# Output projection by one level of Strassen's product, in a gated parallel hybrid encoder layer

## The chip, the cores and the metric

The kernel runs on one core of one Trainium2 chip. The metric is the device time of one execution in microseconds; of several runs the median is given. The profile is that of one execution, and its span reaches from the first to the last instruction.

## The reference, cut to what matters

The layer works on x of 1024 tokens by 1024 channels in float32. One combined projection of the normed x feeds five branches (neighbourhood attention, differential attention, pooling, spatial gating, memory attention) and five gates per channel. The gated branches are summed and pass one output projection:

```python
h = rmsnorm(x, norm_g)
proj = h @ w_in
...
merged = jnp.zeros_like(x)
for i, y in enumerate((y_a, y_b, y_c, y_d, y_m)):
    g_logit = proj[..., SLAB_COLS + i * D_MODEL: SLAB_COLS + (i + 1) * D_MODEL] + b_gate[i]
    merged = merged + jax.nn.sigmoid(g_logit.astype(jnp.float32)).astype(x.dtype) * (y @ w_branch[i])
return x + merged @ w_out
```

So merged and w_out are both 1024 by 1024, and the last product is one of three of that kind of size (the input projection is nine times as wide).

## The kernel before

Every matrix product is made of three: each operand is cut into a coarse part (a cast to fp32r on ScalarE) and a fine part (the difference, on VectorE), and coarse x coarse, coarse x fine and fine x coarse are added in PSUM. `split` does this for activations, `split_w` for weights, in pieces of 128x512.

The normed x is kept transposed in SBUF, in the tiles hh and hl (coarse and fine). `norm_T` makes it by token tiles of 128: load, sum of squares on ScalarE, a reciprocal root by Newton steps on VectorE (`rsqrt_col`), scaling, eight transposes on TensorE, cuts. The weights of w_in come in blocks of 256 columns. Two blocks are held at a time in the slots of wh and wl; `load_w` fills a slot in four pieces as soon as the block before it in this slot has been used. The first two blocks are loaded whole.

The order of the work is the list ORDER of named units, written by hand. A unit emits its instructions; a dash after its name emits the next stage of the same unit. For each engine a scheduler then fixes one fixed queue: it takes the units' position as a priority and goes by its own estimate of when inputs are ready. All loads and stores go from SP's queue, in order, apart from four setup loads on GpSimd's. Units named here: `ld` and `wk` load and norm a token tile, `gn` spreads the norm's gain, `su` is the setup of constants, `bqk`, `bv` are projections of the differential attention, `s` are gate units whose result goes to DRAM early (fillers for TensorE), `mq`, `ma` belong to the memory attention, `g` are the last gate units, which sum a branch into acc.

After the fifth branch of a pair of channel tiles, `merge` cuts acc into mh and ml. Then `out_proj` makes 16 tiles of 128 tokens by 512 columns, each of 8 channel tiles x 3 = 24 matmuls of 128x512, adds x and writes the tile. The left half of w_out is loaded into the two slots (blocks WO0 and WO1), the right half by `load_wo` into the tiles hh0 and hl0, which are free by then; its pieces are cut by ScalarE and VectorE as the first tiles are computed.

## Time and profile before

| | |
|---|---|
| runs, us | 1226.64, 1229.48, 1233.31 |
| median, us | 1229.48 |
| profiled execution, us | 1229.92 |
| its span, us | 1228.1 |
| TensorE, VectorE, ScalarE, GpSimd busy | 98%, 59%, 42%, 12% of the span |
| mean granted clock of TensorE | 0.999 |
| HBM read and written | 103.56 MB and 47.19 MB |

PE is TensorE, PEld its weight loads, DVE VectorE, ACT ScalarE, POOL GpSimd, SP the queue that issues most DMAs. Matmuls overlap, so the busy time of one is longer than the distance from one to the next. Idle time of an engine that is not the bottleneck costs nothing by itself.

### The profile page before, as it was taken

What the parts mean: (1) busy time and instruction counts of PE and PEld (TensorE: products, weight loads), DVE (VectorE), ACT (ScalarE), POOL (GpSimd) and SP (SyncE); (2) the same over time, 40 slices, a digit from 0 to 9 for tenths busy, and PEclk for the clock granted to TensorE, in tenths of its full rate; (3) what the DMA queues carried; (4) which work ended last, traced back from release to release, by engine and by line L of the source; (5) the groups of instructions that cost most, each with busy time, mean ns of one, the idle gap of its engine ahead of it and who ended that gap; (6) DMA issues with size and microseconds to landing.
All of it is one profiled execution on the core that took longest, in us unless ns stands there. A gap on an engine that the chain in (4) does not pass through costs nothing.

```text
span 1228.1 us, 17866 instructions
## 1 busy us (share of the span) xinstructions
PE 1201.9 (98%) x6680; PEld 1031.9 (84%) x6680; DVE 721.5 (59%) x1557; ACT 511.3 (42%) x1033; POOL 144.9 (12%) x150
## 2 busy tenths in 40 slices
PE   7999999999999999999999999999999999999998
PEld 5988888898888898987888898788987777888787
DVE  6865766654476668746655566546555537457411
ACT  5545555434365554334436545535354421113200
POOL 1001111100011111104000001301000004323000
PEclk9999999999999999999999999999999999999999
DMA  6022222113222222333222315835565679562321
GB/s 238 1 87 69 71 74 73 41 48 100 69 80 65 83 86 80 102 107 105 79 86 74 108 44 188 270 129 193 158 218 172 209 267 371 209 232 73 124 97 69
DMA packets 71162, 151.91 MB, mean 124 GB/s; under 512 B 8226, under 2 KB 9794, under 8 KB 71076
## 3 DMA queue, kind: packets, MB, share of 16 engines
q1 hardware_dynamic: 70884, 150.31, 36.4%
q8 instruction: 52, 0.85, 0.3%
q0 software_dynamic: 192, 0.47, 0.1%
q14 instruction: 34, 0.28, 0.1%
HBM read 103.56 MB, written 47.19 MB: 123 GB/s over the span
## 4 chain that ended last, share of the span: by engine, by line
PE 86%; DMA 5%; DVE 4%; ACT 3%; issue 1%; SPq 0%; POOL 0%; DVEq 0%; ACTq 0%; POOLq 0%
PE g L363 15%; PE g L364 15%; PE g L365 15%; PE gz L1000 6%; PE g L349 5%; PE g L351 5%; PE g L350 5%; DMA wr<-in_w_in_dram 3%; PE s L471 3%; PE po L508 2%; PE aT L497 2%; PE g L1090 2%; PE g L1091 2%; PE g L1089 2%; PE ao L906 1%
## 5 line engine op out<-in xcount | busy, mean ns | idle before, releaser
L363 PE MATMUL g<-hh,wh 128*128 128x512 f32 x864 | 342.4, 397 | 3.5 <-ACT gth L984 1.2
L364 PE MATMUL g<-hh,wl 128*128 128x512 f32 x864 | 340.9, 395 | 0.2 <-DVE wl L337 0.2
L365 PE MATMUL g<-hl,wh 128*128 128x512 f32 x864 | 340.8, 394 | 0.0
L363 PEld LDWEIGHTS g<-hh,wh 128*128 128x128 f32 x864 | 162.6, 188 | 35.4 <-ACT gth L984 1.4
L365 PEld LDWEIGHTS g<-hl,wh 128*128 128x128 f32 x864 | 162.6, 188 | 31.8
L364 PEld LDWEIGHTS g<-hh,wl 128*128 128x128 f32 x864 | 162.7, 188 | 31.2 <-DVE wl L337 0.5
L337 DVE TENSOR_TENSOR wl<-wr,wh 128x512 fp32r<-128x512 f32 x148 | 110.9, 753 | 84.8 <-ACT wh L336 84.4
L336 ACT CAST wh<-wr 128x512 fp32r<-128x512 f32 x148 | 91.6, 620 | 156.5 <-DMA wr<-in_w_in_dram 114.9
L349 PE MATMUL g<-wh,hh 128*128 128x256 f32 x512 | 146.9, 288 | 2.6 <-ACT hh L199 1.6
L351 PE MATMUL g<-wh,hl 128*128 128x256 f32 x512 | 146.7, 288 | 0.1
L350 PE MATMUL g<-wl,hh 128*128 128x256 f32 x512 | 146.0, 287 | 0.0
L349 PEld LDWEIGHTS g<-wh,hh 128*128 128x128 f32 x512 | 98.7, 193 | 4.3 <-ACT hh L199 2.7
L1000 PE MATMUL gz<-yh,wb 128*128 128x512 f32 x320 | 100.1, 393 | 2.2 <-DVE gtl L1052 1.9
L351 PEld LDWEIGHTS g<-wh,hl 128*128 128x128 f32 x512 | 98.5, 193 | 1.2 <-issue 0.8
L350 PEld LDWEIGHTS g<-wl,hh 128*128 128x128 f32 x512 | 98.6, 193 | 0.5
L984 ACT ACTIVATE gth<-g,pc 128x512 f32<-128x512 f32 x80 | 55.0, 688 | 99.5 <-PE g L365 76.5
L479 ACT ACTIVATE pB<-s,bmx 128x1024 f32<-128x1024 f32 x64 | 71.6, 1119 | 40.1 <-DVE bmx L477 35.5
L477 DVE TENSOR_REDUCE bmx<-s 128x1 f32<-128x1024 f32 x64 | 77.4, 1217 | 15.2 <-PE s L471 13.0
L485 POOL TENSOR_SCALAR pB<-pB,brc 128x1024 f32<-128x1024 f32 x32 | 38.0, 1189 | 303.6 <-DVE brc L484 196.2
L1000 PEld LDWEIGHTS gz<-yh,wb 128*128 128x128 f32 x320 | 59.3, 188 | 16.0 <-DVE gtl L1052 2.7
L928 POOL TENSOR_TENSOR yy<-yy,yz 128x512 f32<-128x512 f32 x20 | 26.7, 1336 | 332.3 <-DMA yz<-sz 89.1
L1000 PE MATMUL gz<-yl,wb 128*128 128x512 f32 x160 | 62.4, 390 | 0.0
(240 smaller groups left out, 1797.6 us busy)
## 6 DMA issues: line engine op xcount, KB each, us to landing
wr<-in_w_in_dram SPq DMA_DIRECT2D x132, 256.0 KB, 3.4
gs<-gth SPq DMA_DIRECT2D x52, 256.0 KB, 2.0
gtl<-gs SPq DMA_DIRECT2D x26, 512.0 KB, 4.5
wx<-we SPq DMA_DIRECT2D x14, 512.0 KB, 4.0
wb<-wx SPq DMA_DIRECT2D x14, 512.0 KB, 5.7
yx<-ye SPq DMA_DIRECT2D x12, 512.0 KB, 4.3
sz<-zt SPq DMA_DIRECT2D x20, 256.0 KB, 2.0
yz<-sz SPq DMA_DIRECT2D x20, 256.0 KB, 4.1
```

The source lines that it names most:

```text
L336: nc.scalar.copy(out=hi.bitcast(F32R), in_=src)
L337: nc.vector.tensor_tensor(out=lo.bitcast(F32R), in0=src, in1=hi, op=ALU.subtract)
L349: nc.tensor.matmul(out=ps[:, t, :], lhsT=hh[:, ts], rhs=a, start=(i == 0), stop=False)
L350: nc.tensor.matmul(out=ps[:, t, :], lhsT=hh[:, ts], rhs=b, start=False, stop=False)
L351: nc.tensor.matmul(out=ps[:, t, :], lhsT=hl[:, ts], rhs=a, start=False, stop=(i == KT - 1))
L363: nc.tensor.matmul(out=ps, lhsT=a, rhs=hh[:, ts], start=(k == 0), stop=False)
L364: nc.tensor.matmul(out=ps, lhsT=b, rhs=hh[:, ts], start=False, stop=False)
L365: nc.tensor.matmul(out=ps, lhsT=a, rhs=hl[:, ts], start=False, stop=(k == KT - 1))
L477: nc.vector.tensor_reduce(out=nmx[:, m:m + 1], in_=ps, axis=AX.X, op=ALU.max, negate=True)
L479: nc.scalar.activation(out=pe, in_=ps, func=AF.Exp, bias=nmx[:, m:m + 1], accum_out=sums[:, m:m + 1])
L984: nc.scalar.activation(out=tn, in_=ps, func=AF.Tanh, bias=self.bg[:, br, j:j + 1], scale=0.5)
L1000: self.nc.tensor.matmul(out=pz[:, ts], lhsT=wb[:, a, k, cs].bitcast(F32R), rhs=y[b][k][:, ts].bitcast(F32R), start=(i == 0), stop=(i == 5))
```

## The change

The output projection is computed as seven products of half size (Winograd's form of one level of Strassen's scheme), for tokens and output columns in halves, with the channels in halves too. The left operands of four products are sums of quarters of merged, made on VectorE (`s_sums`, and cuts in `sb`, `sd`, `se`) after the last gate unit, in the tiles that h has left. The right operands of four products are sums of quarters of w_out; `t_early` (units wt0 to wt3) makes and cuts them during the memory attention and stores them in DRAM, and `load_o` reads them back. Each product has four tiles of 128x512 with 4 x 3 = 12 matmuls. The units q1, q2, q6, q7, q5, q4, q3 run in this order; P2, P4 and P3 are accumulated in PSUM on top of P1, P7 and P5, and the sums of products are made by VectorE and GpSimd. The stores of the output are issued by ScalarE.

At the start, the fine parts of the first two weight blocks are made by GpSimd (`cut`, units c0 to c7), the setup loads (`sud`) are a unit of their own ahead of the setup's arithmetic, the gain's load goes from ScalarE's queue, and `wk`, `bqk0` and `bv` are divided into more stages. The rest of ORDER is rearranged; `v0.1` is gone, so that these weights are cut when they are used, and `v1.3` is new. The units first, warm0 to warm2 and wp0 to wp7 are defined but do not stand in ORDER. m_norm works its two tiles as one.

```diff
-h ld0 gn ld1 ld2 wk0 id wk0' wk1 L wk1' su ld3 wk3 bst0 ld4 wk2 bvt L wk2' ld5 bqk0.0 wk3' ld6 wk5 wk4 bqk0.0' bv.0
...
-g0.3.1 wo op0.0 op1.0 op0.1 op0.2 op0.4 op1.5 op0.7 op0.6 op1.3 op1.2 op0.5 op0.3 op1.4 op1.6 op1.7 op1.1
+h gn ld0 ld1 wk0 L ld2 wk0' id wk1 wk0'' wk0''' wk1' wk2 c0 c1 c2 c3 sud ld3 wk3 wk1'' ld5 wk1''' bqk0.0 wk3' wk2' su
+bqk0.0' L c4 c5 c6 bvt wk3'' c7 bst0 ld4 wk2'' wk5 ld6 wk2''' wk3''' wk4 bqk0.0'' wk4' wk5' bv.0 bv.0' wk4'' wk4'''
+wk5'' ld7 bqk0.1 wk6 bqk0.1' wk5''' wk6' wk6'' wk6''' wk7 bv.1 wk7' bv.2 bv.1' wk7'' wk7''' bqk0.2 bqk0.2' bv.2'
+bqk0.2'' bqk0.3 bqk0.3' bv.3 bqk0.3'' bv.3' bqk0.1'' s4.2.1.1 ba0.0 ba0.0' ba0.1 ba0.0'' s2.1.0.1 s4.2.0.1 ba0.0'''
...
+du.1 bs0.1' du.3 s4.1.1.0 bs1.1 cl0 bs1.1' dm mn' cl1 ch0 co0 mk co0' ch1 mk' mv co1 mq.0 s0.0.0.1 wt0 mq.1 co1'
+s0.0.1.0 mq.0' avt mq.1' mq.2 mq.2' s0.0.0.0 wt1 mq.3 mq.3' s0.0.1.1 wt2 ma0.0 ma0.1 ma0.0' ma0.0'' av.0.0 ma0.1'
+s0.1.0.0 wt3 av.0.1 ma1.0 s0.1.0.1 ma1.0' ma1.0'' ma2.0 u3.1.0 ma1.1 ma1.1' s0.1.1.0 avx0 ma1.1'' ma0.1'' ma2.0' ma2.1
...
+g2.0.1 w2.2 w2.3 g2.0.0 y4 g2.1.1 g2.2.0 g2.2.1 g2.3.0 w0.2 w4.0 g2.1.0 w4.1 w0.3 g4.0.1 g4.0.0 w4.2 g2.3.1 g4.1.0
+g4.2.0 w4.3 g4.1.1 g4.3.0 w0.0 y0 g4.3.1 w0.1 g0.0.1 g0.1.0 g4.2.1 g0.0.0 g0.1.1 g0.2.0 g0.3.0 g0.2.1 g0.3.1 q1.0 q1.1
+q1.2 q1.3 o6 sa q2.0 q2.1 q2.2 q2.3 sb q6.0 q6.1 q6.2 q6.3 o4 q7.0 q7.1 q7.2 q7.3 sd q5.0 q5.1 q5.2 q5.3 se q4.0 q4.1
+q4.2 q4.3 q3.0 q3.1 q3.2 q3.3
...
+    def setup_loads(self):
+        nc, io, c = self.nc, self.io, self.const
         bc = self.btile("bc")
         cc = self.page("cc")
         nc.gpsimd.dma_start(out=cc[:, 0:384], in_=io["c_mix"])
...
         self.ce = c([P, 32], F32, "ce")
         nc.gpsimd.dma_start(out=self.ce, in_=io["c_edge"])
+        self.early = bc, pv, cc
+
+    def setup(self):
...
-            nc.sync.dma_start(out=row[0:1, :], in_=g.rearrange("(o d) -> o d", o=1))
+            (nc.scalar if early else nc.sync).dma_start(out=row[0:1, :], in_=g.rearrange("(o d) -> o d", o=1))
...
+        def work(i, n=1):
+
+            ss = self.small(n, f"xss{n}")
+            xs, xns = [st.pop(i + j) for j in range(n)], [self.page("xn") for _ in range(n)]
+            for j in range(n):
+                nc.scalar.activation(out=xns[j], in_=xs[j], func=AF.Square, accum_out=ss[:, j:j + 1])
             yield
...
+            r = self.rsqrt_col(ss, n, 1.0 / D, EPS)
+            for j in range(n):
+                nc.vector.scalar_tensor_tensor(out=xns[j], in0=xs[j], scalar=r[:, j:j + 1], in1=st["g"], op0=ALU.mult,
+                                               op1=ALU.mult)
+                yield
+            for j, xn in enumerate(xns):
+                cs = slice((i + j) * P, (i + j + 1) * P)
+                for q in range(2):
+                    ps = self.tbank("xT")
+                    for c in range(4):
+                        k = q * 4 + c
+                        nc.tensor.transpose(out=ps[:, c * P:(c + 1) * P], in_=xn[:, k * P:(k + 1) * P],
+                                            identity=self.ident)
+                    self.split(hi[q][:, :, cs], lo[q][:, :, cs], ps.rearrange("p (a b) -> p a b", a=4))
+                    yield
...
-            v = self.vbig("wv").rearrange("p (k c) -> p k c", k=KT)
+            v = self.big("wv").rearrange("p (k c) -> p k c", k=KT)
         for q in range(4):
             ks = slice(q * 2, q * 2 + 2)
             r = v[:, ks] if whole else self.raw("wr").rearrange("p (k c) -> p k c", k=2)
             nc.sync.dma_start(out=r, in_=src[:, ks])
-            self.split_w(wh[:, ks, :], wl[:, ks, :], r)
+            if whole:
+                self.cuts.append((wh[:, ks, :], wl[:, ks, :], r))
+            else:
+                self.split_w(wh[:, ks, :], wl[:, ks, :], r)
...
+    def cut(self, i):
+        hi, lo, src = self.cuts[i]
+        self.nc.scalar.copy(out=hi.bitcast(F32R), in_=src)
+        self.nc.gpsimd.tensor_tensor(out=lo.bitcast(F32R), in0=src, in1=hi, op=ALU.subtract)
...
         ps = self.gemm_tok(w, tp)
+        if hp == 0:
+            yield
...
+    def b_v(self, w, tp):
+        ps = self.gemm_tok(w, tp)
+        yield
+        for pr in range(2):
+            self.v_split(self.bvt[pr][:, tp * 2:tp * 2 + 2], ps[:, :, pr * P:(pr + 1) * P])
...
+        self.mrg += [(2 * jp + jj, self.acc[jp][:, jj]) for jj in range(2)]
+        for _, a in self.mrg[-2:]:
+            u = self.unit("m1").rearrange("p (x t) -> p x t", x=2)
+            self.s_cut(u, a[:, 0:512])
+            self.m1.append((u[:, 0], u[:, 1]))
+
+    def s_sums(self):
+
+        nc = self.nc
+        self.S = [self.hp.tile([P, 2, 4, 512], F32, name=f"S{i}", tag=t) for i, t in
+                  enumerate(("hh0", "hl0", "hh1", "hl1"))]
+        for k in range(4):
+            a, b = self.mrg[k][1], self.mrg[4 + k][1]
+            a0, a1, b0, b1 = a[:, 0:512], a[:, 512:T], b[:, 0:512], b[:, 512:T]
+            tt = lambda o, x, y, op: nc.vector.tensor_tensor(out=o, in0=x, in1=y, op=op)
+            s1, s2 = self.tmp("s1"), self.ftmp("s2")
+            tt(s1, a1, b1, ALU.add)
+            tt(s2, s1, a0, ALU.subtract)
+            tt(a1, a0, a1, ALU.subtract)
+            tt(a0, b0, s2, ALU.subtract)
+            self.s_cut(self.S[1][:, :, k], s2)
+            self.s_cut(self.S[0][:, :, k], s1)
+
+    def s_cut(self, out, src):
+
+        nc = self.nc
+        nc.scalar.activation(out=out[:, 0].bitcast(F32R), in_=src, func=AF.Copy, scale=0.25)
+        nc.vector.scalar_tensor_tensor(out=out[:, 1].bitcast(F32R), in0=src, scalar=0.25, in1=out[:, 0], op0=ALU.mult,
+                                       op1=ALU.subtract)
+
+    def a22(self, k):
+        u = self.unit("m2").rearrange("p (x t) -> p x t", x=2)
+        self.s_cut(u, self.mrg[4 + k][1][:, 512:T])
+        self.m2.append((u[:, 0], u[:, 1]))
+
+    def t_early(self, k):
+
+        nc = self.nc
+        r = [self.unit("tr").rearrange("p (c n) -> p c n", c=2) for _ in range(2)]
+        for row in range(2):
+            for col in range(2):
+                nc.sync.dma_start(out=r[row][:, col], in_=self.io["w_out"][col][:, self.rows_of[row * 4 + k]])
+        (b11, b12), (b21, b22) = [[x[:, c] for c in range(2)] for x in r]
+        sub = lambda o, x, y: nc.vector.tensor_tensor(out=o, in0=x, in1=y, op=ALU.subtract)
+
+        def out(i, x):
+            u = self.unit("to").rearrange("p (x n) -> p x n", x=2)
+            self.split_w(u[:, 0], u[:, 1], x)
+            if i not in self.tsum:
+                self.tsum[i] = self.dram(f"tsum{i}", (P, 2, 4, 512))
+            nc.sync.dma_start(out=self.tsum[i][:, :, k], in_=u)
+        t = self.ftmp("t1")
+        sub(t, b12, b11)
+        out(5, t)
+        sub(b12, b22, b12)
+        out(7, b12)
+        nc.vector.tensor_tensor(out=b11, in0=b11, in1=b12, op=ALU.add)
+        out(6, b11)
+        sub(b21, b21, b11)
+        out(4, b21)
+
+    def load_o(self, i, slot):
+        nc = self.nc
+        if slot is None:
+            hi, lo = [self.vbig("wo").rearrange("p (k c) -> p k c", k=4) for _ in range(2)]
         else:
-            mh = two(self.big("mh"))
-            ml = two(self.vbig("ml")) if i == 3 else [self.page("ml") for _ in range(2)]
-        for jj in range(2):
-            for th in range(2):
-                ts = slice(th * 512, (th + 1) * 512)
-                a = self.acc[jp][:, jj, ts]
-                nc.scalar.activation(out=mh[jj][:, ts].bitcast(F32R), in_=a, func=AF.Copy, scale=0.25)
-                nc.vector.scalar_tensor_tensor(out=ml[jj][:, ts].bitcast(F32R), in0=a, scalar=0.25,
-                                               in1=mh[jj][:, ts], op0=ALU.mult, op1=ALU.subtract)
-            self.mrg.append((2 * jp + jj, mh[jj], ml[jj]))
-
-    def out_proj(self, w, half, t):
-        nc = self.nc
-        mats = {k: (mh.bitcast(F32R), ml.bitcast(F32R)) for k, mh, ml in self.mrg}
-        xs = self.tmp("xs")
+            hi, lo = [w[:, slot].rearrange("p (k s) c -> p k (s c)", k=4) for w in (self.wh, self.wl)]
+        if i in self.tsum:
+            for x, w in enumerate((hi, lo)):
+                nc.sync.dma_start(out=w, in_=self.tsum[i][:, x])
+        else:
+            row, col = {1: (0, 0), 2: (1, 0), 3: (1, 1)}[i]
+            for k in range(4):
+                r = self.raw("wor")
+                nc.sync.dma_start(out=r, in_=self.io["w_out"][col][:, self.rows_of[row * 4 + k]])
+                self.split_w(hi[:, k], lo[:, k], r)
+        return hi, lo
+
+    def o_prod(self, ps, i, t, w):
+
+        left = {1: self.m1[0:4], 2: self.m1[4:8], 4: self.m2}.get(i)
+        if left is None:
+            S = self.S[{5: 0, 6: 1, 7: 2, 3: 3}[i]]
+            left = [(S[:, 0, k], S[:, 1, k]) for k in range(4)]
+        more = i in (2, 3, 4)
         ts = slice(t * P, (t + 1) * P)
...
+        for k in range(4):
+            ah, al = [x[:, ts].bitcast(F32R) for x in left[k]]
+            bh, bl = [x[:, k].bitcast(F32R) for x in w]
+            for j, (l, r) in enumerate(((ah, bh), (ah, bl), (al, bh))):
+                self.nc.tensor.matmul(out=ps, lhsT=l, rhs=r, start=k + j == 0 and not more, stop=k == 3 and j == 2,
+                                      skip_group_check=more)
+
+    def o_unit(self, i, t, w):
+        nc = self.nc
+        if i in (4, 6):
+            w = self.wx3[i]
+        if i in (1, 7):
+            self.ga[t] = self.bank("oA") if t < 2 else self.tbank("oA")
+        if i in (6, 5):
+            if t % 2 == 0:
+                self.gb = self.sbank("oB")
+            self.ob[t] = self.gb[:, t % 2 * 512:t % 2 * 512 + 512]
+        ps = self.ga[t] if i in (1, 2, 7, 4) else self.ob[t]
+        at = {2: (0, 0), 3: (0, 512), 4: (512, 0), 5: (512, 512)}
+        rows = lambda i: slice(at[i][0] + t * P, at[i][0] + (t + 1) * P)
+        cols = lambda i: slice(at[i][1], at[i][1] + 512)
+        if i in (2, 5):
+            xs = self.tmp("xs")
+            nc.sync.dma_start(out=xs, in_=self.io["x"][rows(i), cols(i)])
+            if i == 5:
+                nc.gpsimd.tensor_tensor(out=xs, in0=xs, in1=self.ov[t], op=ALU.add)
+        elif i in (3, 4):
+            xs = self.xu[t][:, i - 3]
+        elif i == 6:
+            self.xu.append(self.unit("xu").rearrange("p (x n) -> p x n", x=2))
+            for x in range(2):
+                nc.sync.dma_start(out=self.xu[t][:, x], in_=self.io["x"][rows(3 + x), cols(3 + x)])
+        self.o_prod(ps, i, t, w)
+        if i == 1:
+            if t % 2 == 0:
+                u = self.page("ou")
+                self.ou += [u[:, 0:512], u[:, 512:T]]
+            nc.scalar.copy(out=self.ou[t], in_=ps)
+        elif i == 6:
+            nc.vector.tensor_tensor(out=self.ou[t], in0=self.ou[t], in1=ps, op=ALU.add)
+            nc.gpsimd.tensor_tensor(out=self.xu[t], in0=self.xu[t],
+                                    in1=self.ou[t].unsqueeze(1).to_broadcast([P, 2, 512]), op=ALU.add)
+        elif i == 7:
+            if t % 2 == 0:
+                u = self.page("ov")
+                self.ov += [u[:, 0:512], u[:, 512:T]]
+            nc.vector.tensor_tensor(out=self.ov[t], in0=self.ou[t], in1=ps, op=ALU.add)
+        else:
+            for a, b in ((0, 256), (256, 512)) if self.ending else ((0, 512),):
+                nc.vector.tensor_tensor(out=xs[:, a:b], in0=ps[:, a:b], in1=xs[:, a:b], op=ALU.add)
+                nc.scalar.dma_start(out=self.out[rows(i), at[i][1] + a:at[i][1] + b], in_=xs[:, a:b])
+
+    def third(self, i):
+        self.wx3[i] = self.load_o(i, None)
```

## Rows read from the trace of the kernel before

**Rows 1.** The page: busy time of each engine, and the chain that ended last.
```profile
PE 1201.9 (98%) x6680; PEld 1031.9 (84%) x6680; DVE 721.5 (59%) x1557; ACT 511.3 (42%) x1033; POOL 144.9 (12%) x150
...
PE 86%; DMA 5%; DVE 4%; ACT 3%; issue 1%; SPq 0%; POOL 0%; DVEq 0%; ACTq 0%; POOLq 0%
```

**Rows 2.** Waits of TensorE, 0 to 70 us: total, times, longest.
```profile
PE gp L271 <- DMA gb<-in_norm_g_dram: 4.6, 1, 4.6
```

**Rows 3.** Waits of TensorE, 70 to 1130 us: first and last of 17.
```profile
PE gz L1000 <- DVE gtl L1052: 1.9, 2, 1.1
...
PE ao L906 <- DVE aA L200: 0.2, 1, 0.2
```

**Rows 4.** Timeline of the output stage: start, duration, engine, line, operation.
```profile
1134.15 0.39 PE L1089 MATMUL g<-wh,mh 128*128 128x512 f32 x1
...
1224.13 0.39 PE L1091 MATMUL g<-wo,ml 128*128 128x512 f32 x1
...
1225.01 0.81 SPq L1094 DMA_DIRECT2D out_dram<-xs  x2
```

**Rows 5.** Output projection by source line: one of six groups of 64 matmuls.
```profile
L1089 PE MATMUL g<-wh,mh x64: 388/389/501, 1134.2 to 1201.9; 128*128 128x512 f32 x64
```

**Rows 6.** Five stretches: length, busy time of each engine, clock, DMA share, GB/s.
```profile
575.00:670.00 95.00, 94.66 (x609) 85.19 (x608) 55.86 (x137) 45.08 (x99) 8.25 (x4) 1.00 0.27 88
1134.00:1156.00 22.00, 20.74 (x85) 15.22 (x84) 15.48 (x25) 7.98 (x14) 0.00 (x0) 1.00 0.38 118
1156.00:1224.50 68.50, 68.50 (x303) 56.42 (x301) 8.30 (x12) 0.00 (x0) 0.00 (x0) 1.00 0.26 89
7.00:18.20 11.20, 7.67 (x29) 5.66 (x27) 9.72 (x26) 6.62 (x13) 0.00 (x0) 1.00 1.02 382
18.20:66.00 47.80, 45.81 (x384) 44.31 (x384) 40.18 (x134) 24.00 (x51) 5.15 (x22) 1.00 0.08 31
```

**Rows 7.** Timeline of the start, all engines.
```profile
6.65 0.18 DVE L253 TENSOR_SCALAR pc<-pc 128x40 f32<-128x40 f32 x1 [3.45 <-DMA pc<-in_p_col_dram]
...
10.56 2.58 ACT L336 CAST wh<-wv 128x512 fp32r<-128x512 f32 x4 [2.55 <-DMA wv<-in_w_in_dram]
...
13.68 0.58 PE L349 MATMUL g<-wh,hh 128*128 128x256 f32 x1 [1.38 <-ACT hh L199]
...
17.34 0.42 PE L351 MATMUL g<-wh,hl 128*128 128x256 f32 x1
...
17.56 0.42 PE L349 MATMUL g<-wh,hh 128*128 128x256 f32 x1
...
18.56 0.28 PE L349 MATMUL g<-wh,hh 128*128 128x256 f32 x1
```

**Rows 8.** Timeline of VectorE around the first output matmuls.
```profile
1122.77 2.49 DVE L1072 SCALAR_TENSOR_TENSOR ml<-acc,mh 128x512 fp32r<-128x512 f32 x4
...
1140.61 1.29 DVE L1054 TENSOR_TENSOR acc<-acc,gth 128x512 f32<-128x512 f32 x2
```

**Rows 9.** DMA: rate in 40 slices; issues, KB each, us to landing.
```profile
GB/s 238 1 87 69 71 74 73 41 48 100 69 80 65 83 86 80 102 107 105 79 86 74 108 44 188 270 129 193 158 218 172 209 267 371 209 232 73 124 97 69
...
wr<-in_w_in_dram SPq DMA_DIRECT2D x132, 256.0 KB, 3.4
...
yh<-yx SPq DMA_DIRECT2D x6, 512.0 KB, 6.6
...
pv<-in_p_vec_dram POOLq DMA_DIRECT2D x1, 224.0 KB, 7.3
cc<-in_c_mix_dram POOLq DMA_DIRECT2D x1, 192.0 KB, 6.7
```

**Rows 10.** Waits of SP's queue, 575 to 670 us: total, times, longest.
```profile
SPq L321 <- DVE wl L337: 20.3, 10, 3.8
```

**Rows 11.** Two source lines: count, duration in ns min/median/max, forms.
```profile
L193 DVE TENSOR_TENSOR rt<-rt,ra x87: 144/167/1153, 29.8 to 907.8; 128x8 f32<-128x8 f32 x51, 128x16 f32<-128x16 f32 x24, 128x2 f32<-128x2 f32 x12
...
L1054 POOL TENSOR_TENSOR acc<-acc,gth x6: 1285/1298/2295, 1021.1 to 1128.3; 128x512 f32<-128x512 f32 x6
```

More of the change, by code (lines that the diff above doesn't have):

```diff
@@ L1181, in spec, with first, warm @@
         return blocks, units
+    def first(self):
+        last = {}
+        for ins in self.nc.cur_bb.bb.instructions:
+            prev = last.get(ins.engine)
+            if prev is not None:
+                self.tc.add_manual_dep(
+                    ins, prev.name,
+                    mybir.DependencyInfo(mybir.DependencyClass.NoSync, mybir.DependencyReason.DATA),
+                    reason="first")
+            last[ins.engine] = ins
+    def warm(self, i):
+        n = (6, 4, 4)[i]
+        ps = self.bank("warm")
+        for _ in range(n):
+            self.nc.tensor.matmul(out=ps.rearrange("p (a b) -> p a b", a=4), lhsT=self.identr,
+                                  rhs=self.identr.unsqueeze(1).to_broadcast([P, 4, P]), start=True, stop=True)
     def h_begin(self):
@@ L1215, in run @@
                 place[n] = slots.pop(0)
[L1216 to L1217 removed]
+                have[n] = (self.load_o(blocks[n], place[n]) if n[0] == "O" else
+                           self.load_w(blocks[n], place[n], whole=len(have) < 2))
                 if t == "L":
```

170 lines of the change are left out of this document (74 added, 96 removed).

## Prediction, made before the changed kernel ran

> **What bounds the kernel now.** I read the page's busy table first, then the chain that ended last, then TensorE's waits, and last the stretches at both ends. TensorE is busy for 1201.9 of 1228.1 us, VectorE for 59%, ScalarE for 42%; 86% of the chain that ended last is TensorE work [rows 1]. Its waits are short: 4.6 us for the first load is the longest of the start [rows 2], and between 70 and 1130 the largest group is 1.9 us in two pieces [rows 3]. So the sum of TensorE's instructions is nearly the time, and a matmul taken out is time taken out, if nothing else becomes late in its place.
>
> The busy time of one matmul is not its price. Those of 128x512 stand as 0.39 us each [rows 4, 5], but in the undisturbed stretch from 1156 to 1224.5 there is one per 0.226 us (68.5 / 303 [rows 6]); I take 0.227, some records being lost. The first matmul of the output projection starts at 1134.15, the last at 1224.13 [rows 4], and there are six groups of 64, of which one is shown [rows 5]. 384 x 0.227 = 87.2 us; the stage takes 1224.13 + 0.23 - 1134.15 = 90.2, so 3.0 us of it are waits, all before 1156, where TensorE is busy for 20.7 of 22.0 us only [rows 6]. After the last matmul come the output addition in two halves and their DMAs [rows 4]: 1228.1 - 1224.36 = 3.7 us, which stays.
>
> The beginning: the first dense matmul starts at 13.68 and had waited for the cast of hh. That cast stood behind four casts of the first weights on ScalarE, which had waited for their load until 10.56 [rows 7]. The early matmuls of 256 columns start 0.22 us apart and take 0.42, which is 1.2 GHz; at 18.56, after 4.9 us of dense work, one takes 0.28, the upper level [rows 7] (the clock column of the stretch reads 1.00 [rows 6], but it is the matmuls that I go by).
>
> **The change part by part.**
>
> *Seven products for eight.* Before: 16 tiles x 24 = 384 matmuls. After: 7 products x 4 tiles x 12 = 336, of the same shape. 48 x 0.227 = 10.9 us less. This is on the bound; it counts in full unless waits come in.
>
> *The sums of the left side (sa, sb, sd, se).* Each group k takes four additions and two cuts on VectorE, 24 instructions of 128x512 in all. Four of them queued together took 2.49 us [rows 8], which is 0.60 us for each and 0.69 for one alone: 14.4 us. They need the last accumulators. Before, the last one was done at 1140.61 + 1.29 = 1141.9 [rows 8], 7.8 us after the first output matmul (call that T); VectorE was then cutting 16 halves of merged and 8 pieces of w_out. The new merge cuts half as much (8 instructions less) and 4 pieces less stand in this queue: 12 x 0.60 = 7.2 us less. I take it that the sums start near T + 2, and with four cuts of the second weight block and the first additions of q2 between them the last part of the second sum is ready near T + 21. TensorE needs it in q6: q1 and q2 are 96 matmuls, 21.8 us, and its last quarter is read 2 us later, at T + 23.8. So it fits, by some 3 us. The other sums have 10.9 us per product for four cuts each. q1 itself reads only what the two channel pairs that end first have left, and four gate units of 12 products, 10.9 us, stand between their end and q1. Waits of the stage: 2.0 us instead of 3.0, between 0 and 11: gain 1.0.
>
> *Loads of the right sides.* Four of seven come ready cut from DRAM, 2 MB each; each is asked for when a product ends and is needed 21.8 us later. Reads of 512 KB in the busy gate stage landed in 6.6 us; four one behind the other would be 26 us, while at the best rate of a slice, 371 GB/s, 2 MB are 5.7 us [rows 9]. The stage itself used 0.26 to 0.38 of the DMA engines [rows 6]. I take 8 us, hidden. Output DMAs go from ScalarE's queue: 17 issues of some 0.4 us (two in 0.81 on SP [rows 4]), where ScalarE has little left to do after T + 25; if one waits for its addition, the cuts of sb, sd, se behind it wait as well, and have a product's length to do so. Cost 0, and 3 if a cut comes late.
>
> *Sums of w_out early (wt0 to wt3).* 8 MB written, 4 MB read, 16 loads and 16 stores on SP, 32 instructions on VectorE (32 x 0.69 = 22.1 us) and 16 casts on ScalarE (four in 2.58 [rows 7], so 10.3 us), between the pooling branch and the memory attention. In 575 to 670 VectorE is busy for 55.9 of 95 us and ScalarE for 45.1 [rows 6]: they become 78 and 55. TensorE has no idle time to give there, but its filler units do not depend on them. SP is the risk, since a store waits for its cut and the weight loads stand behind it; 20.3 us of the issue of weight loads there are waits for VectorE's cuts now [rows 10]. I charge 1.0 us, between 0 and 24.
>
> *The start.* gn goes first and on ScalarE's queue, the first weights are asked for before the third x tile, and two setup loads (224 and 192 KB [rows 9]) come later. That is 0.9 MB less ahead of the first weights; the stage moves 382 GB/s [rows 6], so 2.4 us at most earlier. The setup arithmetic no longer stands on VectorE ahead of the first norm, where it waited for its load until 6.65 [rows 7]. The eight fine parts of the first weights go from VectorE to GpSimd, 0.69 us each there (5.5 us less for VectorE) and 1.30 us here [rows 11]. TensorE reads one such piece per 6 matmuls of 0.21 to 0.22 us, 1.3 us, so GpSimd just keeps up. First dense matmul: 13.68 - 2.0 = 11.7. The low clock follows the dense work, so it moves with it. Gain 2.0, between -3 and +4 (the upper end takes in the 2.0 us that TensorE is not busy in 18.2 to 66 [rows 6], which finer stages may fill).
>
> What speaks against this move: an instruction of VectorE with two SBUF inputs is held up while GpSimd runs. The same tiny product in a norm takes 0.17 us in the median and 1.15 at most [rows 11], and that longest one stands beside GpSimd's work. The Trainium skill (SBUF — State Buffer, section Who interferes with whom) says why: VectorE and GpSimd share a pair of ports, and whichever comes second blocks for the other's whole instruction when VectorE reads two inputs from SBUF. The trace agrees; taken for every one of the eight, the rule gives the sum of rival C below, 6.5 us in place of 12.9.
>
> *New order.* About 60 units move by a few places; warm and first are defined, but no token calls them. The waits of TensorE between 70 and 1130 are 17 groups of 1.9 down to 0.2 us [rows 3], some 11 us. Any of them may go or come: 0, plus or minus 3.
>
> Sum: 10.9 + 1.0 + 2.0 - 1.0 = 12.9 us. The profiled execution took 1229.92, span 1228.1; the median of the runs is 1229.48, 0.4 less, so I take 1229.9 - 12.9 = 1217.
>
> **The rivals.** A, larger gain: start +4, order +3, no waits at the end (3.0): 10.9 + 3 + 4 + 3 = 20.9, about 1209. For it: VectorE is relieved. Against: its neighbours were already dense. 0.12.
>
> B, q6 waits for its sum. If VectorE runs these at 0.69 and the twelve cuts and additions near them come first, the 36 take 24.8 us from 1141.9: ready at T + 32.6, due at T + 21.8, 10.8 us of wait. For it: VectorE was busy for 15.5 of 22 us from 1134 to 1156 [rows 6], and the accumulators were late by 7.8 us. Against: 7.2 us less ahead of it. With 5 to 11 us of wait the time is 1222 to 1228; middle 1224. 0.20.
>
> C, the port: each of the eight GpSimd cuts holds up one instruction of the norm chain by 1.1 us (1.30 less what it would take itself), 8.9 us in all, against the 7.6 us that VectorE is idle in 18.2 to 66 [rows 6] and the 5.5 taken off. If half comes through to TensorE, the start loses 4.4 instead of gaining 2.0: 1223. 0.10.
>
> D, slower: the w_out sums hold up SP. Each of the four takes 5.5 us of VectorE; with 41% of it free, 13.4 us. If SP stands that long at a store, the loads behind it come 13.4 us late. A block of weights feeds TensorE for 96 x 0.227 = 21.8 us, its four pieces go through two buffers, 3.4 us each to land [rows 9] with the cuts between, some 10, which leaves 11.8. The excess is 1.6 us per sum, 6 in all; with 5.5 each, 22: 1229.9 - 13.9 + 22 = 1238. It decides for slower from 5.0 us each. Against: the weight loads in these 95 us are few, ten of them with such a wait [rows 10], and a store can be issued late. 0.08.
>
> **How the numbers follow.** Forecast 0.50: gain 9 to 17, 1213 to 1221. A 0.12, B 0.20, C 0.10, D 0.08. The bound of telling a change is 0.5%, 6.1 us: below 1223.3. Faster: 0.50 + 0.12 + 0.08 of B + 0.07 of C = 0.77. Slower: 0.05 of D. Same: 0.18. The range 1208 to 1226 leaves out the end of A, the worst of B and D.
>
> **What would show it.** Right: 336 matmuls of the new product line 0.227 us apart and a stage of about 78 us from its first to its last; no wait over 2 us in front of the sixth product; first dense matmul near 11.7; TensorE's waits in 575 to 670 as small as now. Wrong: a gap at q6 with VectorE's sums as the releaser (B); norm instructions of over 1 us before 40 us and TensorE behind them (C); weight casts that wait for their load in 575 to 670 and TensorE behind those (D); a stage that is short and a time that isn't, then the loss is in the order of the middle.

## The result, and the profile after

The changed kernel takes 1213.44 us, the median of 4 runs (1213.25 to 1214.93); the kernel before took 1231.11 beside it (4 runs, 1226.64 to 1233.31). The ratio is 0.9861, with a 95% interval of 0.9844 to 0.9878: 17.7 us faster, where 12.9 were forecast. The same program, measured a second time (experiment 4), gave 1211.79 (0.9850, 0.9828 to 0.9872). Sign and range of the prediction hold; the sum came out 5 us too small, and the sections below find which terms those are.

The page after, busy time of each engine and the chain that ended last:

```profile
PE 1187.2 (98%) x6632; PEld 1025.2 (85%) x6632; DVE 753.6 (62%) x1608; ACT 525.8 (43%) x1061; POOL 171.3 (14%) x166
...
PE 87%; DMA 5%; DVE 4%; ACT 2%; issue 1%; POOL 0%; SPq 0%; DVEq 0%; POOLq 0%; ACTq 0%
```

Against [rows 1], TensorE has 48 instructions and 14.7 us of busy time less and is as large a part of the chain. VectorE gained 32 us of work, ScalarE 14, GpSimd 26, and their shares of the chain did not grow. The span fell from 1228.1 to 1213.1 us.

The output stage, as a timeline of TensorE and then of the end (start, duration, engine, line, operation), and as a stretch of line L1183 alone (length, busy time of TensorE and of its weight loads, clock, DMA share, GB/s):

```profile
1133.04 0.39 PE L1183 MATMUL oA<-wh,m 128*128 128x512 f32 x1
...
1208.74 0.39 PE L1183 MATMUL oB<-wh,S 128*128 128x512 f32 x1
1209.17 0.76 DVE L1228 TENSOR_TENSOR xu<-oB,xu 128x256 f32<-128x256 f32 x2 [2.03 <-PE oB L1183]
```

```profile
1133.04:1209.00 75.96, 75.96 (x335) 62.69 (x334) 1.00 0.62 229
```

From 1133.04 to 1208.97 is 75.9 us, and TensorE is busy in every hundredth of it: 335 matmuls (one of the 336 stands earlier, at 1127.37) and no wait. Before, this stage took 90.2 us, 3.0 of them waits [rows 4, 6]. So the stage gives 14 us and more: 10.9 from the products taken out, 3.0 from waits. The tail after the last matmul is 4.1 us (3.7 before). What is left, 1.1 us in this execution, lies ahead of 1133. In the second profiled execution of the same program the first of the unbroken output matmuls starts at 1129.68, 4.5 us ahead of [rows 4]: the part ahead of the stage is also the part that differs between executions of one program.

TensorE's waits from 70 to 1130 us (total, times, longest), in after:

```profile
PE g L383 <- DVE mv L476: 2.4, 1, 2.4
PE g L369 <- ACT sq L395: 1.6, 1, 1.6
PE cps L709 <- ACT sq L395: 1.2, 1, 1.2
PE g L371 <- DVE mTl L206: 1.2, 1, 1.2
...
PE aS L904 <- DVE gth L1048: 0.2, 1, 0.2
```

The first line says that a matmul of line 383 waited once, 2.4 us, for VectorE's piece of mv, the values of the memory attention; mTl is the fine part of the normed memory, sq the squares for a norm, gth and gtl are gates. There are 12 groups, where before had 17 [rows 3]; the largest of before, gz for gtl, is not among them, and mv and mTl are new. These two and the 1.2 us for sq stand at 575 to 600 us. The other waits for sq are at 264 and 764 us, where before has shorter ones (0.6 and 0.9). Three of before's four largest stand at 820 to 1050 us, the one for gtl and these (there alone):

```profile
PE g L363 <- ACT gth L984: 1.2, 1, 1.2
PE aS L875 <- DVE amx L880: 0.9, 1, 0.9
```

So the new waits are not the waits of before made smaller: they are in another place.

The start, from the timeline of all engines:

```profile
6.25 1.04 ACT L290 ACTIVATE xn<-xt 128x1024 f32<-128x1024 f32 x1
...
9.27 1.28 DVE L294 SCALAR_TENSOR_TENSOR xn<-xt,cy,gp 128x1024 f32<-128x1024 f32 x1
9.85 3.72 POOL L352 TENSOR_TENSOR wl<-wv,wh 128x512 fp32r<-128x512 f32 x3 [2.97 <-DMA wv<-in_w_in_dram]
...
10.46 0.68 DVE L318 SCALAR_TENSOR_TENSOR cu<-cy,ca 128x1 f32<-128x1 f32 x1
10.69 1.94 PE L303 MATMUL xT<-ident,xn 128*128 128x128 f32 x8 [4.58 <-DVE xn L294]
11.18 1.19 DVE L322 SCALAR_TENSOR_TENSOR cy<-cu,cy 128x1 f32<-128x1 f32 x1
...
12.41 1.19 DVE L318 SCALAR_TENSOR_TENSOR cu<-cy,ca 128x1 f32<-128x1 f32 x1
...
12.80 1.05 ACT L205 CAST hh<-xT 128x512 fp32r<-128x512 f32 x2
13.41 0.58 PE L369 MATMUL g<-wh,hh 128*128 128x256 f32 x1 [0.78 <-ACT hh L205]
...
15.47 1.28 DVE L206 TENSOR_TENSOR hl<-xT,hh 128x512 fp32r<-128x512 f32 x2
...
16.21 1.12 PE L303 MATMUL xT<-ident,xn 128*128 128x128 f32 x4 [2.00 <-DVE hl L206]
16.98 0.56 PE L371 MATMUL g<-wh,hl 128*128 128x256 f32 x1
```

The first dense matmul starts at 13.41, not 11.7. After two of them TensorE stands idle for 2.0 us for hl, and the first matmul that reads hl starts at 16.98. Beside GpSimd's three cuts (9.85 to 13.57) three tiny steps of the norm take 0.68, 1.19 and 1.19 us, where the same lines take 0.16 and 0.22 a moment later; so hl, due right after hh, is made at 15.47. Matmuls of 256 columns take 0.41 us until 21.2 and 0.27 from 21.56; in [rows 7] one takes 0.28 at 18.56. That is rival C's mechanism, in full view. These rows agree with the rule of the Trainium skill that the prediction weighed (SBUF — State Buffer, section Who interferes with whom).

### The profile page after: what moved, and what is told of

Read it like the earlier page. It is cut to its first block, busy times and chain, and to the rows that moved or that the text cites. A ratio compares the mean times of both kernels' runs of the same rounds, so it can differ in the third digit from the quotient of the medians.

```text
span 1213.1 us, 17945 instructions
## 1 busy us (share of the span) xinstructions
PE 1187.2 (98%) x6632; PEld 1025.2 (85%) x6632; DVE 753.6 (62%) x1608; ACT 525.8 (43%) x1061; POOL 171.3 (14%) x166
## 4 chain that ended last, share of the span: by engine, by line
PE 87%; DMA 5%; DVE 4%; ACT 2%; issue 1%; POOL 0%; SPq 0%; DVEq 0%; POOLq 0%; ACTq 0%
PE g L383 15%; PE g L384 15%; PE g L385 15%; PE gz L1029 8%; PE g L371 5%; PE g L369 5%; PE g L370 5%; PE oA L1183 4%; PE oB L1183 3%; PE s L499 3%; PE po L536 3%; PE aT L525 2%; DMA wr<-in_w_in_dram 2%; DMA yz<-sz 1%; PE ao L935 1%
## 5 line engine op out<-in xcount | busy, mean ns | idle before, releaser
L357 DVE TENSOR_TENSOR wl<-wr,wh 128x512 fp32r<-128x512 f32 x140 | 104.6, 752 | 78.5 <-ACT wh L356 77.8
L356 ACT CAST wh<-wr 128x512 fp32r<-128x512 f32 x140 | 86.9, 622 | 137.8 <-DMA wr<-in_w_in_dram 105.8
L507 ACT ACTIVATE pB<-s,bmx 128x1024 f32<-128x1024 f32 x64 | 71.7, 1120 | 31.0 <-DVE bmx L505 28.7
```

Source lines behind the costliest of these rows:

```text
L356: nc.scalar.copy(out=hi.bitcast(F32R), in_=src)
L357: nc.vector.tensor_tensor(out=lo.bitcast(F32R), in0=src, in1=hi, op=ALU.subtract)
L507: nc.scalar.activation(out=pe, in_=ps, func=AF.Exp, bias=nmx[:, m:m + 1], accum_out=sums[:, m:m + 1])
```

## The experiments

Theory after the traces: products 10.9, waits of the output stage 3.0, and the rest a balance of the start, of the early sums' cost at 575 to 620 us and of the order's gain at 820 to 1050. Rivals: the terms on record, and rival C for the start. Times are medians beside the kernel before on the same chip (1230.5 to 1230.9), ratios to it with their interval.

**1. Only the seven products, in the old order.** Start, norm stages and order of before; the output stage and wt0 to wt3 of after.

```diff
-mq.0 co1 s0.0.0.1 s0.0.1.0 mq.1 ... g0.3.1 wo op0.0 ...
+mq.0 co1 s0.0.0.1 wt0 s0.0.1.0 mq.1 ... g0.3.1 q1.0 ...
```

> Only the output projection in seven products with its early sums, put into the kernel before: start, norm stages and order of the middle are those of before, the early sums stand beside the same units as in after. Against the kernel before: the terms on record (10.9 product, 1.0 waits, minus 1.0 early sums) expect 10.9 us faster, about 7 us slower than after. The theory from the trace of after (10.9 product, 3.0 waits, minus 4 to 5 early sums, with 3 of start and 4 to 5 of order missing) expects 9 to 10 us faster than before, 8 us slower than after. If the start of after is a loss (rival C) and the order gives nothing, it is as fast as after or faster.

Measured: 1221.21, ratio 0.9930 (0.9911 to 0.9949), 9.3 us faster than before, within 6.3 to 11.0. That is what the theory from the trace expected; the 10.9 of the terms on record lies in that interval too, so the run does not tell the two apart. It is clearly slower than after.

**2. The old start with all the rest of after.**

```diff
-h gn ld0 ld1 wk0 L ld2 wk0' ... (finer stages, cuts on GpSimd)
+h ld0 gn ld1 ld2 wk0 id wk0' ... bv.3  (as before, with its functions)
 s4.2.1.1 ba0.0 ba0.0' ...              (as after)
```

> The changed kernel with the start of before (loads, constants, norm stages, cuts of the first two weight blocks on VectorE and the order up to the first score block), and the new order behind it. The term on record (start gains 2.0) expects it 2 us slower than after; the work counted in the trace of after (about 3 us ahead of before at 120 us) expects 3 us slower; rival C (the start loses 4.4 us to GpSimd's cuts) expects 4 us faster than after.

The norm's functions are those of before too, so m_norm works its two tiles one by one again.

Measured: 1211.19, ratio 0.9845 (0.9827 to 0.9863). It is neither 2 to 3 us slower nor 4 faster than after (1213.44 and 1211.79): the whole new start is worth nothing that can be measured.

**3. The new order alone, eight products.**

```diff
 h ld0 gn ld1 ... bv.3                  (as before)
+s4.2.1.1 ba0.0 ... g0.3.1              (order of after, no wt)
 wo op0.0 op1.0 ...                     (as before)
```

> The kernel before, eight products and its own start, with only the new order of the units from the first score block to the last gate unit (without the early sums, which it has no use for). With it there are four corners: old or new order, eight or seven products. Theory: the order alone takes the TensorE waits of 820 to 1050 us (about 5 of them named in the chain of before) away; it is 4 to 6 us faster than before, with those waits gone from the trace, and the seven products are worth 13 to 15 us on top. Rival: the new order only repairs what the early sums and the new merge disturb (the old order with seven products had lost more there than before); then it is within 2 us of before. The term on record (0, plus or minus 3) holds up to 3 us.

Measured: 1226.61 (10 runs), ratio 0.9968 (0.9954 to 0.9982): 2.2 to 5.7 us faster, 4 by the ratio. So there are four corners, and the trace has a row for each. One stretch, 500 to 1126 us, ahead of the output stage; the second and third number are its length and TensorE's busy time.

Before (old order, eight products):

```profile
500.00:1126.00 626.00, 616.25 (x3397) 528.58 (x3396) 359.26 (x823) 250.43 (x553) 78.14 (x50) 1.00 0.48 161
```

Experiment 1 (old order, seven):

```profile
500.00:1126.00 626.00, 613.11 (x3375) 525.83 (x3375) 372.95 (x847) 256.76 (x564) 79.27 (x50) 1.00 0.53 181
```

Experiment 3 (new order, eight):

```profile
500.00:1126.00 626.00, 619.50 (x3419) 534.51 (x3418) 357.15 (x818) 252.52 (x555) 81.66 (x53) 1.00 0.48 162
```

Experiment 2 (new order, seven):

```profile
500.00:1126.00 626.00, 618.69 (x3423) 534.17 (x3422) 377.53 (x849) 258.77 (x569) 83.41 (x55) 1.00 0.53 180
```

TensorE is idle for 9.8, 12.9, 6.5 and 7.3 us of the 626. In the old order the seven products bring 3.1 us of idle time with them: 1.9 more at 575 to 670 us, where the early sums are made, 2.5 more at 820 to 1050, and some less elsewhere. In the new order they bring 0.8. The order takes 3.3 us of idle time away with eight products and 5.6 with seven. The measured times say the same, larger: the order is worth 4.3 us with eight products (1230.9 to 1226.6) and 10.0 with seven (1221.2 to 1211.2; 5.9 between the nearest ends of the two intervals, against 5.7 at most with eight); the products are worth 9.3 in the old order and 15.4 in the new. So the theory held, at the lower end of its range for the order and a little above it for the products, and the terms of the sum were not independent. Of the 5.7 us by which they differ, idle time between 500 and 1126 us is 2.3. Another part is the clock: in experiment 1, behind waits of 0.9 and 1.4 us at 930 to 932 us, matmuls of 128x512 take 0.63 us until 934.9, the lower level, and 0.39 from 936.45. Where the rest lies is open, since short stretches at the lower level are in the traces of experiments 2 and 3 as well, in other places (479 and 596 us).

**4. The changed kernel once more**, unedited, as the scale for experiments 6, 9 and 10, measured beside it.

> The changed kernel once more, unedited, as the scale for the three edits of one or two places measured beside it, and for how much the time of one program differs between chips. Expected: 0.986 of the kernel before, within 0.002; the TensorE waits of 2.4 us at 593 us and of about 2 us at 14 us are there again.

Measured: 1211.79, ratio 0.9850 (0.9828 to 0.9872). Two measurements of one program are 1.6 us apart, so edits that give 1211 to 1214 are told from neither. The wait of 2 us at 14 us is there again; the one for mv is 1.7 us, not 2.4. The matmuls behind it, in after and in this execution:

```profile
595.36 0.77 PE L383 MATMUL g<-hh,wh 128*128 128x512 f32 x1 [2.39 <-DVE mv L476]
...
597.21 0.63 PE L384 MATMUL g<-hh,wl 128*128 128x512 f32 x1
```

```profile
594.41 0.47 PE L383 MATMUL g<-hh,wh 128*128 128x512 f32 x1 [1.67 <-DVE mv L476]
...
594.95 0.39 PE L385 MATMUL g<-hl,wh 128*128 128x512 f32 x1
```

Behind the 2.4 us the next matmuls stand 0.43 us apart until 598, the lower level (granted clock 0.96 from 575 to 620 us); behind the 1.7 us they stand 0.23 apart (granted clock 1.00). Here the first execution loses 0.7 us by the longer wait and 1.4 by the clock, 2.1 of the 3.3 us between the two spans. So a wait can cost more than its idle time. Its length alone does not tell whether it will: in experiment 5 matmuls take 0.63 us from 972.1 to 974.7, behind a wait of 1.7 us.

**5. The old order in the last third only**, from at3 to the last gate unit, in the changed kernel.

```diff
-at3 aa3.0 w1.3 aa3.3 aa3.0' ... aa3.2'''' aa3.3'''' g3.0.1 ... w0.0 y0 g4.3.1 ...
+at3 aa3.0 aa3.3 w1.3 aa3.0' ... g3.0.1 aa3.2'''' ... y0 w4.3 ... w0.0 g4.3.1 ...
```

> The changed kernel with the order of the units from the token at3 to the last gate unit (about 900 to 1130 us) as in the kernel before; the one branch-weight load that only before makes early stays as in after. If the gain of the order sits in this stretch, 4 to 7 us slower than after, with TensorE waits for gth, gtl and amx at 920 to 1020 us as in before. If it sits ahead of it, or comes from the weight load that is prepared early, less than 2 us.

Measured: 1220.51, ratio 0.9911 (0.9897 to 0.9926): 7 to 9 us slower than after. Its waits of TensorE from 820 to 1050 us:

```profile
PE gz L1029 <- DVE gtl L1081: 3.7, 3, 1.7
PE aT L926 <- DVE ay L944: 1.7, 1, 1.7
```

Experiment 1 has the first of them too, with others of its kind (820 to 1130 us):

```profile
PE g L366 <- ACT gth L993: 2.0, 2, 1.2
PE gz L1009 <- DVE gtl L1061: 1.7, 2, 1.0
PE aS L884 <- DVE amx L889: 1.6, 2, 0.9
PE gz L1009 <- DVE gth L1028: 1.4, 1, 1.4
```

In after only 1.5 us of named waits are left there; 0.7 for aA is the largest. From 820 to 1050 us TensorE is idle for 6.8 us in experiment 5 and 1.9 in after, and about 1.5 us go to the matmuls at the lower level (experiment 4). So this third is where most of what the order is worth with seven products lies. How it pays is read from the rows, no run took it apart: the branch products (gz) wait for the gate products (gtl, gth) and the last attention for its row maxima (amx), and these are queued on VectorE among the cuts of weights. Of the three expected names only gtl came back; ay came in place of amx and gth. The longest wait for gtl (until 1013.92) stands behind a cut on VectorE that took 2.29 us in place of 0.69, beside an addition on GpSimd:

```profile
1009.20 2.40 POOL L1083 TENSOR_TENSOR acc<-acc,gtl 128x1024 f32<-128x1024 f32 x1 [93.72 <-DVE gtl L1081]
...
1009.86 2.29 DVE L357 TENSOR_TENSOR wl<-wr,wh 128x512 fp32r<-128x512 f32 x1 [0.74 <-ACT wh L356]
```

That is what rival C describes, in a place where the prediction did not look for it.

**6. The old order from 500 to 620 us only.** After's waits for mTl, sq and mv at 575 to 600 us looked like a loss by the new order.

```diff
-ds s3.1.0.1 s3.0.1.0 dv.0 mn dv.1 ... co0 mk co0' ch1 mk' mv co1 mq.0 ... ma0.0
+ds s3.1.0.1 s3.0.1.0 dv.0 dv.1 ... mn dv.2 ... co0 co0' ch1 mk mk' mv mq.0 co1 ... ma0.0
```

> The changed kernel with the order of the units from the token ds to ma0.0 (about 500 to 620 us) as in the kernel before, the early sums beside the same units. The theory: the new order of the memory and convolution branches costs 4 to 5 us at 573 to 600 us (waits of 1.4, 1.2 and 2.4 us for mTl, sq and mv), which an order-independent reading puts on the early sums. With the old order these waits fall under 1 us each and the kernel is 3 to 5 us faster than after. Rivals: the early sums cause them, then they stay (0); or what is gained here is waited for again later, at 640 to 820 us (0 to 2).

Measured: 1215.00, ratio 0.9873 (0.9851 to 0.9895); not faster, and by the medians 3 us slower than the unedited kernel beside it. The waits named are gone, as expected, and come back elsewhere: from 500 to 1126 us TensorE is busy for

```profile
500.00:1126.00 626.00, 615.54 (x3396) 528.63 (x3395) 373.12 (x844) 256.80 (x565) 80.06 (x52) 1.00 0.53 180
```

10.5 us idle, against 8.0 and 9.4 in the two executions of after. My theory of that place falls; the largest named wait of the kernel is not an invitation to undo its order.

**7. No early sums of w_out.** One block loaded, cut and stored four times stands for all.

```diff
 def t_early(self, k):
+    if k:
+        return
...
+    self.split_w(u[:, 0], u[:, 1], r[:, 0])
+    for c in range(4):
+        nc.sync.dma_start(out=d[:, :, c], in_=u)
+    self.tsum = {i: d for i in (4, 5, 6, 7)}
...
-        sub(t, b12, b11)
-        out(5, t)
...
```

> The changed kernel with the early sums of w_out left out: one block of w_out is loaded and cut once, and this cut block is stored four times in one DRAM tile that products 4 to 7 all read (their right sides are not the sums, so the output is not the reference's; the loads of products 4 to 7 keep their size). Left out are 15 of 16 loads, all 16 subtractions and additions, 15 of 16 cuts and 12 of 16 stores. Against the changed kernel (1213.4 us): the theory on record (early sums cost 1.0 us) expects about 1212.4. The theory from the trace of after (TensorE's 2.4 us wait at 593 us and the others near it come from the early sums) expects 1208 to 1210. The rival that these waits come from the new order of the stage around 575 to 600 us expects 1213 with the 2.4 us wait still there.

Measured: 1211.12, ratio 0.9850 (0.9831 to 0.9868): within what two measurements of after differ by. From 575 to 670 us:

```profile
575.00:670.00 95.00, 90.98 (x580) 81.55 (x580) 56.88 (x136) 44.38 (x92) 7.42 (x4) 1.00 0.30 100
```

VectorE falls back to 56.9 us, near to [rows 6], and TensorE's 4.0 us of idle time stay (4.8 and 4.4 in after). So this idle time is the new order's. Experiment 3, with that order and neither the early sums nor the norm of after, has the same waits (1.7, 1.2 and 1.1 us for mv, sq and mTl) and 4.1 us. The early sums cost TensorE 0.4 to 0.8 us there.

**8. The first cuts on VectorE in place of GpSimd.**

```diff
-        self.nc.gpsimd.tensor_tensor(out=lo.bitcast(F32R), in0=src, in1=hi, op=ALU.subtract)
+        self.nc.vector.tensor_tensor(out=lo.bitcast(F32R), in0=src, in1=hi, op=ALU.subtract)
```

> The changed kernel with the eight low-part subtractions of the first two weight blocks on VectorE in place of GpSimd. If GpSimd's subtractions hold VectorE's small operations up (0.68 to 1.19 us each at 10.5 to 13.6 us where others take 0.16 to 0.22), these come back to about 0.2 us, the first dense matmul moves from 13.4 to about 12 us, and the whole is 1 to 2 us faster than after. The rival, that VectorE is the bound of the start and eight more instructions of 0.69 us fall on it, expects 0 to 3 us slower.

Measured: 1211.60, ratio 0.9846 (0.9831 to 0.9860). The steps of the norm are short again, and hl comes 2.3 us sooner:

```profile
12.77 0.22 DVE L318 SCALAR_TENSOR_TENSOR cu<-cy,ca 128x1 f32<-128x1 f32 x1
...
13.22 0.69 DVE L206 TENSOR_TENSOR hl<-xT,hh 128x512 fp32r<-128x512 f32 x1
...
17.29 0.28 PE L371 MATMUL g<-wh,hl 128*128 128x256 f32 x1
```

The matmuls reach the upper level at 17.29 in place of 21.56. The first dense matmul is at 13.24, not 12, and the time is not told from after's. How much of the start comes through is read from one instruction, the first matmul after the wait for glr, which all these kernels have near 465 us, behind the same number of matmuls. In after and experiment 10, which have the same start:

```profile
465.86 0.39 PE L369 MATMUL g<-wh,hh 128*128 128x256 f32 x1 [0.63 <-ACT glr L576]
```

```profile
464.03 0.39 PE L369 MATMUL g<-wh,hh 128*128 128x256 f32 x1 [0.63 <-ACT glr L576]
```

In experiments 8 and 9, both with the cuts on VectorE:

```profile
464.61 0.39 PE L369 MATMUL g<-wh,hh 128*128 128x256 f32 x1 [0.63 <-ACT glr L576]
```

```profile
466.10 0.50 PE L382 MATMUL g<-hh,wh 128*128 128x512 f32 x1 [0.63 <-ACT glr L575]
```

The eight profiled executions with the start of after lie between 464.03 and 465.86, the four with the start of before between 464.69 and 465.62. So by 465 us nothing is left of the 2.3 us that hl had come sooner. The 4.3 us of the upper level were in part the execution's: in the eight it comes between 18.4 and 21.7, with the cuts on VectorE at 17.3 and 18.4. From 18.2 to 66 us TensorE is idle for 0.6 us in after, for 2.1 in experiment 8 and for 2.0 before [rows 6]; what starts late waits less.

**9. Edits 6 and 8 together.**

> Both edits: the order of 500 to 620 us as in before and the eight first cuts on VectorE. If the two losses are independent the gains add: 5 to 7 us faster than after. If the stages between absorb one of them (queues full at 120 to 500 us), it is as fast as the better of the two alone.

Measured: 1213.59, ratio 0.9866 (0.9842 to 0.9891): as after. Nothing adds up, since neither part is a gain.

**10. The first product on the last blocks.** The left sides of products 1 and 2 exchanged.

```diff
-        left = {1: self.m1[0:4], 2: self.m1[4:8], 4: self.m2}.get(i)
+        left = {2: self.m1[0:4], 1: self.m1[4:8], 4: self.m2}.get(i)
```

> The changed kernel with the left sides of products 1 and 2 exchanged, so that the first product needs the blocks that are merged last (the two products then hold other numbers, the work is the same). The theory: the 3.0 us of TensorE waits at the head of the output stage of before (2.2 us of them at 1134 us) are gone because the first product needs only blocks merged long before; the exchange then brings 2 to 3 us of waits back at about 1131 us and makes the kernel that much slower. The rival, that they are gone because the last merge is half as long and output blocks no longer wait for other stores, expects under 0.7 us of waits and no change that can be measured. The term on record (waits of 2.0 us stay) expects no difference between the two.

Measured: 1213.52, ratio 0.9856 (0.9833 to 0.9879), no difference. One wait comes back in 1120 to 1170 us:

```profile
PE oA L1183 <- DVE m L1120: 0.7, 1, 0.7
```

So the early blocks of the first product are worth 1 us at most, and my theory of the vanished waits falls. In before, TensorE's weight loads in the same stretch waited longest for the cuts of w_out, which stood on VectorE beside the last merges:

```profile
PEld g L1090 <- DVE wo L337: 2.1, 3, 1.0
PEld g L1091 <- DVE ml L1072: 1.0, 3, 0.4
```

In after the first products need four cut pieces of w_out each instead of eight per half, and four of the seven right sides come cut from DRAM. That this is the cause is read from the rows, no run took it apart. It is a matter of the seven products and not of the order: experiment 3, new order and eight products, still has 1.9 us of such waits of TensorE (for wo and ml), experiment 1, old order and seven products, has none.

**11. The sums' cuts twice.**

```diff
+            for _ in range(2):
                 self.s_cut(self.S[1][:, :, k], s2)
                 self.s_cut(self.S[0][:, :, k], s1)
```

> The changed kernel with the eight cuts of the first two left-side sums made twice (same numbers): 8 more instructions of 0.60 to 0.69 us on VectorE and 8 more on ScalarE between the first output matmul and the sixth product, 5 us of VectorE. The step on record has the second sum ready some 3 us ahead of its need: then TensorE waits about 2 us ahead of the sixth product and the kernel is 1 to 3 us slower than after. Rival B's sum, in which there is no slack, expects the whole 5 us. If the slack is larger than 5 us: no wait, no difference.

Measured: 1216.62, ratio 0.9879 (0.9861 to 0.9896), 3 to 5 us slower by the medians. The output stage takes 78.5 us in place of 75.9. Product 6, which reads the second sum, does not make TensorE wait (its weight loads stand 0.2 us for S); two products later, at 1178, there is a wait. From 1170 to 1220 us:

```profile
PE oB L1184 <- DVE ou L1219: 1.9, 1, 1.9
```

VectorE's queue, 5 us longer, is late for product 6's addition, which frees the bank of PSUM that product 5 takes. That q6 does not wait is no sign of 5 us of slack: the scheduler, which fixes the queues anew for each kernel, put ten matmuls of product 7 behind the first four of product 6 (in after product 6 goes on for 16). In after the slack can be read: the last cut of the second sum ends at 1155.06, and the first matmul that reads it, the twelfth of product 6, starts at 1157.06. That is 2 us at most; the step on record had some 3.

**12. The stores on SP's queue.**

```diff
-                nc.scalar.dma_start(out=self.out[rows(i), ...
+                nc.sync.dma_start(out=self.out[rows(i), ...
```

> The changed kernel with the stores of the output on SP's queue in place of ScalarE's. The step on record charges ScalarE's queue nothing; then there is no difference, or up to 1 us slower where a store that waits for its addition holds up a load behind it. If the stores on ScalarE delay the cuts behind them, it is 1 to 3 us faster.

Measured: 1211.70, ratio 0.9847 (0.9832 to 0.9861), and no wait in the output stage: no difference.

## Why the prediction was right, and which of its terms were not

Faster by more than 0.5% was the likeliest case, and 1213.4 lies in the range, at the lower edge of the forecast's own 1213 to 1221; the second measurement, 1211.79, lies just outside that and still in the range. That the sum is no further off is in part luck: the start's 2.0 did not come, and 2.0 more came from waits that it had kept. Term by term:

*Seven products for eight, 10.9:* right. 48 matmuls fewer on the bound, and every one counts: 335 in 75.9 us is 0.227 each.

*Left-side sums, waits of 2.0 us in place of 3.0:* too careful by 2 us. The waits are all gone (gain 3.0). The prediction had no row for the 2.0 that it let stay. The count of VectorE's queue up to q6 was right: 3 us of slack forecast, 2 read (experiment 11). Rival B did not come, but it was 2 us away.

*Right sides and stores, 0:* right (experiment 12, and no wait in the stage).

*Sums of w_out early, minus 1.0:* right for the kernel as changed (experiment 7, about half a microsecond). In the old order TensorE is idle for 1.9 us more in that stretch, and there rival D shows, small: in experiment 1 TensorE waits 1.5 us at 646 to 652 us for weight cuts (wh, wl). In after weight loads wait for VectorE's cuts as they did (19.8 us, [rows 10]), and TensorE does not stand behind them.

*Start, plus 2.0:* wrong; nothing can be measured (experiment 2). The step put the first dense matmul on the first weights' load. In before the casts of these weights hold up the first cast of hh, as they stand ahead of it in ScalarE's queue; x is not far behind:

```profile
4.58 1.06 ACT L278 ACTIVATE xn<-xt 128x1024 f32<-128x1024 f32 x1 [1.30 <-DMA xt<-in_x_dram]
...
10.36 1.94 PE L286 MATMUL xT<-ident,xn 128*128 128x128 f32 x8 [2.01 <-DVE cu L300]
...
13.05 0.58 ACT L199 CAST hh<-xT 128x512 fp32r<-128x512 f32 x1
```

Eight transposes took 1.94 us, so the first four, all that the first cast of hh reads, were done near 11.4 (an estimate, half of that row). The cast began at 13.05, so an earlier load had some 1.6 us to give, if nothing else came into ScalarE's queue. Something did. In after three casts of weights are over at 11.08, and then ScalarE squares the third x tile, which is now asked for behind the first weights:

```profile
11.74 1.06 ACT L290 ACTIVATE xn<-xt 128x1024 f32<-128x1024 f32 x1 [0.67 <-DMA xt<-in_x_dram]
```

So hh is cast at 12.80, 0.25 us sooner and no more. The first x tile comes later too: its square starts at 6.25 instead of 4.58, because a piece of the weights is asked for ahead of it. GpSimd's cuts then stretch the norm behind it. The low clock did not simply move along with the first dense matmul: it lasted 4.5 us behind it before and 5.1 to 8.6 us in the eight executions of this start. And yet all of it is made up by 465 us. I had rival C's mechanism with a price of 4.4; the mechanism is there, and no price of it can be measured (experiment 8).

*New order, 0 plus or minus 3:* this is the step that failed most. Alone it is worth 4 us (2.2 to 5.7), and with the seven products 10. The waits between 70 and 1130 that I summed as "some 11 us" and let go either way are not a pool of chance: those of 820 to 1050 us go with the last third of the order, and come back with it (experiment 5, 7 to 9 us). That they have one cause, VectorE's queue, is argued from the rows.

Sum as measured: 10.9 + 3.0 + 4 for the order alone - 0.5 for the early sums + 0 for the start = 17.4 us, against 17.7 and 18.8 in the two measurements. The agreement should not be read too closely: this takes the order at its price without the new products, and the products at a price (13.4) between those measured in the two orders (9.3 and 15.4).

What stays open: which of the places moved in the last third matters, since all of it was put back at once; which part of the seven products took away the stage waits; where all of the 5.7 us lie by which order and products are worth more together; and why the wait for mv, and with it the clock behind it, differs from one execution of one program to the next.

## What to carry to other kernels

Where one engine is 98% busy, price a removed product by its pitch, the distance from one matmul to the next, in an undisturbed stretch; the pitch came back as it was taken, 0.227 us. Price a new order and the work that it has to carry together: measured as four corners, the order was worth 4 us without the new work and 10 with it, and the product 9 without the new order and 15 with it. And a wait is not a price: the largest wait of the changed kernel's middle (2.4 us at 593) and its late start (2.3 us for hl) could be undone without a gain that can be measured, since TensorE waited elsewhere instead. Nor is one execution a scale: with one and the same start the same matmul came at 464.03 and at 465.86 us, further apart than many of these edits are worth.

## What the runs showed of the hardware that was not expected

A norm step of 128x1 on VectorE took 1.19 us beside GpSimd's cut and 0.22 when the cut stood on VectorE itself, and a cut of 128x512 took 2.29 us beside an addition on GpSimd. That the whole start, with hl 2.3 us later and the matmuls at the lower level until 18.4 to 21.7 in place of 17.3 and 18.4, comes to nothing by 465 us was not expected. Two profiled executions of one program had 9.4 and 8.0 us of idle TensorE in the same 626 us, and spans of 1213.1 and 1209.8; in the first, matmuls fell to the lower level behind a wait of 2.4 us and took 1.4 us longer for it, in the second they stayed at the upper level behind 1.7 us.
